# Pooling mixer of a decoder trunk: the 16 meta tokens as the last rows of a whole 128-token tile, and both halves of z scaled before the first pooled tile

## The chip, the cores and the metric

The kernel runs on one core of a Trainium2 chip. The metric is the device time in microseconds of one execution. Engines are named as the profile names them: PE is TensorE's matmul, PEld its weight load, DVE is VectorE, ACT is ScalarE, POOL is GpSimd, SP is SyncE. L558 is line 558 of the kernel before. PEclk is the clock that TensorE was granted, as a share of 2.4 GHz; it has two levels here, 1.00 (2.4 GHz) and 0.50 (1.2 GHz).

## What is computed

A trunk of two layers over 272 tokens of 1024 features: 256 tokens of the sequence and 16 learned meta tokens ahead of them, which are dropped at the end. Each layer is SwiGLU FFN, mixer, SwiGLU FFN, each with an RMS norm before and after it. The mixer of layer 0 is the causal pooling mixer, on which the change works:

```python
def causal_multiscale_pool(h, w, b, scale):
    cs = jnp.pad(jnp.cumsum(hf, axis=1), ((0, 0), (1, 0), (0, 0)))
    ...
    for g, win in enumerate(POOL_WINDOWS):          # 2, 4, 8, 16
        lo = jnp.maximum(t + 1 - win, 0)
        cnt = (t + 1 - lo).astype(jnp.float32)
        pooled.append((csg[:, 1:, g] - csg[:, lo, g]) / cnt[None, :, None])
    ...
    diff = (pooled - hg).astype(h.dtype)
    y = jnp.einsum('blgc,gcd->blgd', diff, w) + b   # four groups of 256 features
    return y.reshape(bsz, L, D) * scale
...
hn = rmsnorm(h, mix_norm_pre[i])
m = causal_multiscale_pool(hn, pool_w[j], pool_b[j], pool_scale[j])
h = h + rmsnorm(m, mix_norm_post[i])
```

The mixer of layer 1 is a differential attention, which the change leaves alone.

## The kernel before

The residual `h` stays on the chip, features on partitions: eight tiles `h[j]` of 128 features by 272 tokens. Columns 0 to 255 are the tokens of the sequence, columns 256 to 271 the 16 meta tokens, so that the meta tokens, first in time, stand last in a tile.

The order of work on PE, ACT, DVE and SP is written out by hand, and each engine runs its instructions in that order. Every stage follows the one before: FFN 0, the pooling mixer, FFN 1, FFN 2, the attention, FFN 3. An FFN has `first_blocks` (the first three of 22 blocks of the hidden layer, eight feature tiles one after the other, L416), the other up-products and the down-products (L216 to L218: each product in three passes over halves `hi` and `lo` of both operands). The weights are loaded by SP into `raw`, and ACT and DVE split them into `whi` (L101) and `wlo` (L114), some units ahead.

`pool_mix` works between FFN 0 and FFN 1, in full f32, where the trace shows two passes of PE for each product:

1. PE fills the time until the first `h[j]` with twelve products on constants (`warm`, L230), while DVE finishes the norm of FFN 0 and adds it to `h` (L569, L570).
2. `inner(j)`, L558: z = h^T w, for feature tile j and each token tile. Group g = j // 2 takes two tiles j. The token tiles are `tok`: columns 0 to 127, 128 to 255, and 256 to 271, so the third has 16 rows. `z[q][ti]` is a PSUM bank for half q of the features (j 0 to 3, j 4 to 7) and token tile ti. `inner(0)` to `inner(5)` come first, then L581, which sums the squares of each token into `sums` (three token tiles), then `inner(6)` and `inner(7)`.
3. `r2`: the reciprocal root of `sums`, in ACT (L242) and DVE (L236 to L238).
4. `normed(q)`: half q of z, scaled by r2 and copied into SBUF as `zs[0]` (ACT, L591), `zs[1]` (DVE, L592) and `zs[2]` (16 rows; ACT for q = 0, L596, DVE for q = 1, L594).
5. `pooled(j)`: PE multiplies columns j of `zs[1]`, `zs[0]` and `zs[2]` with the band matrices `bands` (L604, L605, L608) into one PSUM bank y of 128 features by 272 tokens. The third product has 16 rows of operand and writes the first 16 tokens and the meta tokens. ACT squares y (`post.squared`, L378), DVE sums the squares (L389). For j = 0, 3, 4 DVE also scales y at once (L371).
6. Three more `warm` products, then the norm's sum (`post.rms`, L395 and L396), its root (ACT, L242), and FFN 1 begins with L273 and L275 on DVE, which make the first operand `xhi`. The other scaled y are made by ACT then (L362, L373); that gives the banks free into which `first_blocks` writes.

What stands where in time is set by this loop, which the change replaces:

```python
for q in range(2):
    normed(q)
    for j in range(4 * q, 4 * q + 4):
        pooled(j)
        if j == 0:
            first(0)
        if j in EARLY:
            scaled(j, True)
```

Of the kernel before, what the change touches and what calls it, by code (L numbers as in the profile page):

```python
# [12 lines left out]
ALU = mybir.AluOpType  # L13
# [3 lines left out]
P = 128  # L17
D = 1024
NK = D // P
NMETA = 16  # L20
SEQ = 256
L = NMETA + SEQ
# [35 lines left out]
EARLY = (0, 3, 4)  # L58
# [86 lines left out]
def trunk(ctx, tc, ht, w13a, w13b, w2t, w2n, wqkva, wqkv, wo, wp, vec, lamv, mask, band, gpost, out):  # L145
    nc = tc.nc
# [11 lines left out]
    wps = []  # L158
# [381 lines left out]
    def pool_mix(old, ps, post):  # L540

        def bank():
            return ps.tile([P, 512], F32, tag="bank", name="bank")

        tok = ((0, P), (P, 2 * P), (2 * P, L))
        rows = (P, P, NMETA)

        z = [[bank() for _ in rows] for _ in range(2)]
        sums = bank()[:, 0:3]
        idle = bank()  # L550
        nc.vector.memset(sums, 0.0)
        warm(lambda: idle, ones, WARM0, P)
        old.refine()

        def inner(j):
            g = j // 2
            for ti, m in enumerate(rows):
                nc.tensor.matmul(z[g // 2][ti][:m, (g % 2) * 256:(g % 2 + 1) * 256],  # L558
                                 lhsT=h[j][:, tok[ti][0]:tok[ti][1]], rhs=wps[j], start=j % 2 == 0, stop=j % 2 == 1)

        with tc.tile_pool(name="poolw", bufs=1, reuse_waits="tile") as pw:
# [17 lines left out]
            nc.vector.tensor_tensor(acc[:, 0], acc[:, 0], acc[:, 1], ALU.add)  # L579
            for ti, m in enumerate(rows):  # L580
                nc.tensor.matmul(sums[:m, ti:ti + 1], lhsT=acc[:, 0, tok[ti][0]:tok[ti][1]], rhs=ones[:, 0:1],  # L581
                                 start=True, stop=True)
            for j in range(NK - LATE, NK):
# [5 lines left out]
            def normed(q):  # L589
                at = slice(q * 512, (q + 1) * 512)  # L590
                nc.scalar.mul(out=zs[0][:, at], in_=z[q][0], mul=r2[:, 0:1])  # L591
                nc.vector.tensor_scalar(zs[1][:, at], z[q][1], r2[:, 1:2], None, ALU.mult)  # L592
                if q:
                    nc.vector.tensor_scalar(zs[2][:NMETA, at], z[q][2][:NMETA], r2[:NMETA, 2:3], None, ALU.mult)  # L594
                else:
                    nc.scalar.mul(out=zs[2][:NMETA, at], in_=z[q][2][:NMETA], mul=r2[:NMETA, 2:3])  # L596

            def pooled(j):
# [8 lines left out]
                ends = y.rearrange("p (a b) -> p a b", b=SEQ)[:, :, 0:NMETA]  # L607
                nc.tensor.matmul(ends, lhsT=zs[2][:NMETA, c],  # L608
                                 rhs=bands[:NMETA, g, P + NMETA:].rearrange("p (a b) -> p a b", b=NMETA),
                                 start=False, stop=True, skip_group_check=True)  # L610
# [4 lines left out]
            def scaled(j, vector=False):  # L615
                post.scaled(j, ys[j][:, :L], pbg[:, j:j + 1], vector)

            def first(j):
                post.new(j, ys[j][:, :L], pfirst[:, j:j + 1], pfirst[:, NK + j:NK + j + 1])

            for q in range(2):
                normed(q)
                for j in range(4 * q, 4 * q + 4):
                    pooled(j)
                    if j == 0:
                        first(0)
                    if j in EARLY:
                        scaled(j, True)
            s = bank()
# [417 lines left out]
def _layout(x, meta_tokens, ffn_norm_pre, ffn_norm_post, ffn_w1, ffn_w3, ffn_w2, mix_norm_pre, mix_norm_post,  # L1047
# [9 lines left out]
    def first(a):  # L1057

        n = a.shape[0]
        a = a.transpose(0, 2, 1, 3, 4).reshape(n, P, 6, 8 * P)  # L1060
        return c(a.transpose(0, 2, 1, 3))
# [30 lines left out]
    ends = np.zeros((P, 4, 2 * NMETA))  # L1092
    ends[:NMETA] = np.where((d >= 0) & (d < win), 1.0 / count, 0.0) - (d == 0)
    r["band"] = c(np.concatenate([inside, ends], axis=2).astype(np.float32))
# [22 lines left out]
```

## Time and profile before

| | |
|---|---|
| three runs | 977.39, 979.08 and 979.39 us; median 979.08 us |
| profiled execution | 979.49 us, its span 977.4 us |
| PE busy | 958.1 us, 98% of the span |
| DVE, ACT busy | 602.7 us (62%), 500.4 us (51%) |
| mean granted clock of PE | 0.987 |
| HBM read | 158.56 MB, 163 GB/s over the span |

The busy times of the engines overlap, and a busy PE can be one at half its clock. The time of the execution is 2.1 us over its span.

### The profile page before, as it was taken

The page shows a single profiled execution, that of the slowest core. Times are in us where ns is not written, and L with a number is a line of the kernel's source. Part 1 is how long each engine was busy: PE and PEld are TensorE (multiplying, and loading weights), DVE is VectorE, ACT ScalarE, POOL GpSimd, SP SyncE. Part 2 cuts the span into 40 slices and gives each one's busy share as a digit, 9 for nine tenths or more (in the row PEclk, how much of TensorE's full clock was granted, in tenths as well). Part 3 has the DMA queues.
Part 4 walks back from the last instruction along what each step waited for, and adds up shares of the span by engine and source line. Part 5 has one row for each costly group of instructions (what it writes and reads, how often), then busy time and mean ns, then how long its engine had stood idle before and what let it go on. Part 6 is the DMA issues. An engine that isn't in the chain of part 4 may idle for free.

```text
span 977.4 us, 17910 instructions
## 1 busy us (share of the span) xinstructions
PE 958.1 (98%) x7242; PEld 923.0 (94%) x7242; DVE 602.7 (62%) x1029; ACT 500.4 (51%) x851; POOL 10.8 (1%) x18
## 2 busy tenths in 40 slices
PE   9999999998999999999999999999999999999997
PEld 8999999976999999999999999999997899999996
DVE  6855554453885555446955554458876788555553
ACT  7744454434564445543744455435776766444432
POOL 0000000200000000000000000000000000000000
PEclk9999999997899999999999999999999999999999
DMA  8765557630175556551665556532523538655521
GB/s 294 249 209 180 166 161 220 214 98 0 45 267 185 174 163 180 177 194 44 229 211 179 169 161 189 184 116 88 170 89 113 196 102 298 194 177 179 187 87 43
DMA packets 48322, 160.77 MB, mean 164 GB/s; under 512 B 5488, under 2 KB 9456, under 8 KB 48240
## 3 DMA queue, kind: packets, MB, share of 16 engines
q1 hardware_dynamic: 47952, 159.45, 50.8%
q8 instruction: 56, 0.92, 0.4%
q10 hardware_dynamic: 288, 0.19, 0.1%
q14 instruction: 26, 0.21, 0.1%
HBM read 158.56 MB, written 1.05 MB: 163 GB/s over the span
## 4 chain that ended last, share of the span: by engine, by line
PE 96%; ACT 1%; DVE 1%; DMA 1%; SPq 1%; issue 0%; DVEq 0%; ACTq 0%
PE bank L218 27%; PE bank L216 27%; PE bank L217 27%; PE bank L416 9%; PE bank L558 1%; DMA raw<-in_w13a 1%; PE bank L739 1%; ACT whi L101 0%; PE bank L604 0%; PE bank L230 0%; SPq L79 0%; PE bank L737 0%; PE bank L608 0%; PE bank L748 0%; PE bank L671 0%; PE bank L670 0%
## 5 line engine op out<-in xcount | busy, mean ns | idle before, releaser
L114 DVE TENSOR_TENSOR wlo<-raw,whi 128x1024 fp32r<-128x1024 f32 (+3 forms) x308 | 361.3, 1177 | 59.9 <-PE bank L217 28.3
L216 PE MATMUL bank<-xhi,whi 128*128 128x272 f32 (+1 forms) x1360 | 390.4, 287 | 0.0
L218 PE MATMUL bank<-xlo,whi 128*128 128x272 f32 (+1 forms) x1360 | 389.9, 287 | 0.0
L217 PE MATMUL bank<-xhi,wlo 128*128 128x272 f32 (+1 forms) x1360 | 388.6, 286 | 0.1
L101 ACT CAST whi<-raw 128x1024 fp32r<-128x1024 f32 (+3 forms) x308 | 306.7, 1011 | 54.9 <-PE bank L218 47.2
L216 PEld LDWEIGHTS bank<-xhi,whi 128*128 128x128 f32 x1360 | 255.8, 188 | 1.1 <-issue 0.4
L217 PEld LDWEIGHTS bank<-xhi,wlo 128*128 128x128 f32 x1360 | 255.7, 188 | 1.0 <-DVE wlo L114 0.3
L218 PEld LDWEIGHTS bank<-xlo,whi 128*128 128x128 f32 x1360 | 256.1, 188 | 0.0
L218 PE MATMUL bank<-glo,whi 128*128 128x272 f32 x528 | 152.3, 288 | 0.0
L216 PE MATMUL bank<-ghi,whi 128*128 128x272 f32 x528 | 152.1, 288 | 0.0
L217 PE MATMUL bank<-ghi,wlo 128*128 128x272 f32 x528 | 151.5, 287 | 0.0
L454 ACT ACTIVATE ua<-ua 128x272 f32<-128x272 f32 (+1 forms) x88 | 37.1, 429 | 143.5 <-DVE ua L449 143.5
L217 PEld LDWEIGHTS bank<-ghi,wlo 128*128 128x128 f32 x528 | 99.3, 188 | 0.0
L216 PEld LDWEIGHTS bank<-ghi,whi 128*128 128x128 f32 x528 | 99.2, 188 | 0.0
L218 PEld LDWEIGHTS bank<-glo,whi 128*128 128x128 f32 x528 | 99.0, 188 | 0.0
L460 DVE TENSOR_TENSOR ua<-bank,ua 128x272 f32<-128x272 f32 (+1 forms) x88 | 37.6, 435 | 95.0 <-PE bank L218 95.0
L463 ACT CAST ghi<-ua 128x272 fp32r<-128x272 f32 (+1 forms) x88 | 36.1, 417 | 112.0 <-DVE ua L460 112.0
L449 DVE TENSOR_TENSOR ua<-bank,ny 128x272 f32<-128x272 f32 (+1 forms) x88 | 37.6, 435 | 89.6 <-PE bank L218 89.5
L416 PE MATMUL bank<-xhi,whi 128*128 128x272 f32 (+1 forms) x240 | 40.5, 306 | 7.8 <-DVE xhi L275 6.2
L416 PEld LDWEIGHTS bank<-xhi,whi 128*128 128x128 f32 x240 | 34.9, 202 | 11.1 <-DVE xhi L275 6.3
L389 DVE TENSOR_TENSOR pacc<-pacc,sq 128x272 f32<-128x272 f32 (+1 forms) x31 | 13.6, 439 | 45.0 <-ACT sq L378 44.9
L378 ACT ACTIVATE sq<-bank 128x272 f32<-128x272 f32 (+1 forms) x32 | 12.8, 400 | 55.7 <-PE bank L218 55.7
(178 smaller groups left out, 894.1 us busy)
## 6 DMA issues: line engine op xcount, KB each, us to landing
raw<-in_w13b SPq DMA_DIRECT2D x152, 512.0 KB, 4.0
raw<-in_w2t SPq DMA_DIRECT2D x48, 448.0 KB, 3.3
raw<-in_w2t SPq DMA_DIRECT2D x24, 512.0 KB, 3.6
raw<-in_w2n SPq DMA_DIRECT2D x22, 512.0 KB, 3.5
raw<-in_w13a SPq DMA_DIRECT2D x21, 512.0 KB, 4.2
raw<-in_wqkv SPq DMA_DIRECT2D x18, 512.0 KB, 3.9
raw<-in_wo SPq DMA_DIRECT2D x8, 512.0 KB, 3.5
raw<-in_wqkva SPq DMA_DIRECT2D x6, 512.0 KB, 3.8
```

Source lines behind the costliest of these rows:

```text
L101: self.nc.scalar.copy(out=hi[:, at], in_=self.raws[u][:, at])
L114: self.nc.vector.tensor_tensor(lo[:, at], raw[:, at], hi[:, at].bitcast(F32), ALU.subtract)
L216: nc.tensor.matmul(out_ap, lhsT=a[0], rhs=b[0], start=start, stop=False)
L217: nc.tensor.matmul(out_ap, lhsT=a[1], rhs=b[0], start=False, stop=False)
L218: nc.tensor.matmul(out_ap, lhsT=a[0], rhs=b[1], start=False, stop=stop)
L378: nc.scalar.activation(out=sq[:, :n], in_=y, func=AF.Square, scale=scale, bias=bias)
L389: nc.vector.tensor_tensor(acc[:, :n], self.acc[:, :n], sq[:, :n], ALU.add)
L416: nc.tensor.matmul(us[q][:, :n], lhsT=taken[u][a][:, c * P:(c + 1) * P], rhs=x[:, :n], start=start, stop=stop)
L449: nc.vector.tensor_tensor(a[:, :self.n], u1[:, :self.n], self.r2[:, :self.n], ALU.mult)
L454: nc.scalar.activation(out=a[:, :self.n], in_=a[:, :self.n], func=AF.Silu)
L460: nc.vector.tensor_tensor(s[:, :n], u3[:, :n], s[:, :n], ALU.mult)
L463: nc.scalar.copy(out=hi, in_=s[:, :n])
```

## The change

The third token tile becomes columns 144 to 271, a whole tile of 128 tokens, of which the meta tokens are the last 16 rows. Its products in `inner` and its sums of squares have 128 rows in place of 16, its scaled copy `zs[2]` has 128 rows, and the third band product has 128 rows of operand. The band for it holds its values in rows 112 to 127, and zeros in the 112 rows above. The `memset` of `sums` goes. And `normed(0)` and `normed(1)` both stand ahead of the first `pooled(j)`, whose order stays.

```diff
-        tok = ((0, P), (P, 2 * P), (2 * P, L))
-        rows = (P, P, NMETA)
-
-        z = [[bank() for _ in rows] for _ in range(2)]
+        tok = ((0, P), (P, 2 * P), (L - P, L))
+
+        z = [[bank() for _ in tok] for _ in range(2)]
         sums = bank()[:, 0:3]
         idle = bank()
-        nc.vector.memset(sums, 0.0)
...
-            for ti, m in enumerate(rows):
-                nc.tensor.matmul(z[g // 2][ti][:m, (g % 2) * 256:(g % 2 + 1) * 256],
-                                 lhsT=h[j][:, tok[ti][0]:tok[ti][1]], rhs=wps[j], start=j % 2 == 0, stop=j % 2 == 1)
+            for ti, (t0, t1) in enumerate(tok):
+                nc.tensor.matmul(z[g // 2][ti][:, (g % 2) * 256:(g % 2 + 1) * 256],
+                                 lhsT=h[j][:, t0:t1], rhs=wps[j], start=j % 2 == 0, stop=j % 2 == 1)
...
-                    nc.vector.tensor_scalar(zs[2][:NMETA, at], z[q][2][:NMETA], r2[:NMETA, 2:3], None, ALU.mult)
+                    nc.vector.tensor_scalar(zs[2][:, at], z[q][2], r2[:, 2:3], None, ALU.mult)
                 else:
-                    nc.scalar.mul(out=zs[2][:NMETA, at], in_=z[q][2][:NMETA], mul=r2[:NMETA, 2:3])
+                    nc.scalar.mul(out=zs[2][:, at], in_=z[q][2], mul=r2[:, 2:3])
...
-                nc.tensor.matmul(ends, lhsT=zs[2][:NMETA, c],
-                                 rhs=bands[:NMETA, g, P + NMETA:].rearrange("p (a b) -> p a b", b=NMETA),
+                nc.tensor.matmul(ends, lhsT=zs[2][:, c],
+                                 rhs=bands[:, g, P + NMETA:].rearrange("p (a b) -> p a b", b=NMETA),
...
-            for q in range(2):
-                normed(q)
-                for j in range(4 * q, 4 * q + 4):
-                    pooled(j)
-                    if j == 0:
-                        first(0)
-                    if j in EARLY:
-                        scaled(j, True)
+            normed(0)
+            normed(1)
+            for j in range(NK):
+                pooled(j)
+                if j == 0:
+                    first(0)
+                if j in EARLY:
+                    scaled(j, True)
...
-    ends[:NMETA] = np.where((d >= 0) & (d < win), 1.0 / count, 0.0) - (d == 0)
+    ends[P - NMETA:] = np.where((d >= 0) & (d < win), 1.0 / count, 0.0) - (d == 0)
```

On PE, from the last token tile of `inner(5)` to the first pooled tile, the kernel before issues these (the size is that of the result, so 16x256 is a product for the meta tile; zs_2596 is `zs[1]`, zs_2595 `zs[0]`, zs_2597 `zs[2]`):

```order
L558 MATMUL bank<-wp,h 16x256
L581 MATMUL bank<-ones,pacc_2633 128x1 x2
L581 MATMUL bank<-ones,pacc_2633 16x1
L558 MATMUL bank<-wp,h 128x256 x2
L558 MATMUL bank<-wp,h 16x256
L558 MATMUL bank<-wp,h 128x256 x2
L558 MATMUL bank<-wp,h 16x256
L604 MATMUL bank<-bands,zs_2596 128x128
L605 MATMUL bank<-bands,zs_2595 128x144
L608 MATMUL bank<-bands,zs_2597 128x2x16
```

The changed kernel issues this from `inner(0)` to the first pooled tile (L557 is `inner`, L580 the sums, L602, L603 and L606 the band products, zs_2595 `zs[1]`, zs_2594 `zs[0]`, zs_2596 `zs[2]`):

```order
L557 MATMUL bank<-wp,h 128x256 x18
L580 MATMUL bank<-ones,pacc_2632 128x1 x3
L557 MATMUL bank<-wp,h 128x256 x6
L602 MATMUL bank<-bands,zs_2595 128x128
L603 MATMUL bank<-bands,zs_2594 128x144
L606 MATMUL bank<-bands,zs_2596 128x2x16
```

The number of products and their order are the same; no product with 16 rows or 16 result rows is left.

On DVE, from the root of the sums into the pooled tiles, before:

```order
L238 SCALAR_TENSOR_TENSOR ny<-nt,ny 128x3
L592 TENSOR_SCALAR zs_2596<-bank,ny 128x512
L371 TENSOR_SCALAR bt<-bank,psg,pbg 128x272
L389 TENSOR_TENSOR pacc<-sq 128x272
L389 TENSOR_TENSOR pacc<-pacc,sq 128x272
L371 TENSOR_SCALAR bt<-bank,psg,pbg 128x272
L592 TENSOR_SCALAR zs_2596<-bank,ny 128x512
L594 TENSOR_SCALAR zs_2597<-bank,ny 16x512
```

and in the changed kernel:

```order
L238 SCALAR_TENSOR_TENSOR ny<-nt,ny 128x3
L590 TENSOR_SCALAR zs_2595<-bank,ny 128x512 x2
L592 TENSOR_SCALAR zs_2596<-bank,ny 128x512
L371 TENSOR_SCALAR bt<-bank,psg,pbg 128x272
L389 TENSOR_TENSOR pacc<-sq 128x272
```

The two copies of half 1 (`zs[1]` and `zs[2]`) moved from behind two scaled tiles and two sums of squares to directly behind the copy of half 0.

On ACT, the same place before:

```order
L242 ACTIVATE ny<-bank,eps_c 128x3
L591 ACTIVATE zs_2595<-bank,ny 128x512
L596 ACTIVATE zs_2597<-bank,ny 16x512
L378 ACTIVATE sq<-bank,pbs,vt 128x272
L362 ACTIVATE b<-bank,pfirst 128x272
L378 ACTIVATE sq<-bank,pbs,vt 128x272 x3
L591 ACTIVATE zs_2595<-bank,ny 128x512
L378 ACTIVATE sq<-bank,pbs,vt 128x272 x4
```

and in the changed kernel:

```order
L242 ACTIVATE ny<-bank,eps_c 128x3
L589 ACTIVATE zs_2594<-bank,ny 128x512
L594 ACTIVATE zs_2596<-bank,ny 128x512
L589 ACTIVATE zs_2594<-bank,ny 128x512
L378 ACTIVATE sq<-bank,pbs,vt 128x272
L362 ACTIVATE b<-bank,pfirst 128x272
L378 ACTIVATE sq<-bank,pbs,vt 128x272 x7
```

The copy of half 1 moved from behind the fourth square to ahead of the first.

## Rows read from the trace of the kernel before

**Rows 1.** The page: the granted clock of PE in 40 equal slices of the span (tenths of full speed).

```profile
PEclk9999999997899999999999999999999999999999
```

**Rows 2.** Busy time of each engine by stretch, around the end of the mixer: the stretch, its length, busy us of PE, PEld, DVE, ACT and POOL (instructions), the granted clock, DMA share and GB/s.

```profile
225.00:230.00 5.00, 4.72 (x27) 3.36 (x26) 1.44 (x3) 2.45 (x5) 0.00 (x0) 1.00 0.00 0
230.00:235.00 5.00, 3.36 (x14) 2.81 (x15) 3.12 (x6) 1.81 (x4) 0.00 (x0) 0.74 0.00 2
240.00:245.00 5.00, 3.47 (x10) 2.03 (x8) 2.78 (x7) 3.40 (x8) 0.00 (x0) 0.50 0.00 0
245.00:250.00 5.00, 5.00 (x25) 5.00 (x25) 4.16 (x12) 2.06 (x5) 0.00 (x0) 0.55 0.02 3
```

**Rows 3.** The chain of work that ended last, in order of time, from the fourth pooled tile to the start of FFN 1: start, us, what.

```profile
229.75 0.59 ACT sq L378
...
230.37 0.56 DVE bt L371
230.93 0.67 DVE zs L592
...
231.64 0.49 PE bank L604 x2
...
241.60 0.50 ACT ny L242
...
242.12 0.45 DVE rt L273
...
242.60 0.45 DVE xhi L275
...
243.09 16.94 PE bank L416 x107
```

**Rows 4.** Timelines and groups of `inner`, L558. First PE: the start, length and number of passes of `inner(0)` to `inner(5)`; two passes of the second token tile's neighbourhood in `inner(1)`; the line's passes with shortest, median and longest ns. Then PEld, the weight loads of `inner(1)`, of which 128*16 is the meta tile's, with the idle time before them; and the loads of the whole stage by shape (busy us, mean ns, idle before).

```profile
212.24 9.62 PE L558 MATMUL bank<-wp,h 128*128 128x256 f32 x36 [0.46 <-issue]
...
214.13 0.59 PE L558 MATMUL bank<-wp,h 128*128 128x256 f32 x2
...
L558 PE MATMUL bank<-wp,h x48: 379/379/483, 212.2 to 225.3; 128*128 128x256 f32 x32, 128*16 128x256 f32 x16
...
214.87 0.11 PEld L558 LDWEIGHTS bank<-wp,h 128*16 128x16 f32 x2 [0.33 <-issue]
215.40 0.73 PEld L558 LDWEIGHTS bank<-wp,h 128*128 128x128 f32 x4 [0.42 <-issue]
...
L558 PEld LDWEIGHTS bank<-wp,h 128*128 128x128 f32 x32 | 5.4, 189 | 3.6 <-issue 3.2
L558 PEld LDWEIGHTS bank<-wp,h 128*16 128x16 f32 x16 | 0.9, 94 | 2.7 <-issue 2.7
```

**Rows 5.** Timeline of PE: the first product of pooled tiles 0, 1, 6 and 7, so that from row to row a whole tile of six passes lies between.

```profile
225.65 0.49 PE L604 MATMUL bank<-bands,zs 128*128 128x128 f32 x2
...
226.65 0.49 PE L604 MATMUL bank<-bands,zs 128*128 128x128 f32 x2
...
234.57 0.80 PE L604 MATMUL bank<-bands,zs 128*128 128x128 f32 x2
...
236.34 0.80 PE L604 MATMUL bank<-bands,zs 128*128 128x128 f32 x2
```

**Rows 6.** Timeline of PE at a granted clock of 1.00: the two products of a norm's sum, 24 passes of 128 columns on one weight shape, and the sums of squares (six passes of one column).

```profile
207.73 0.62 PE L395 MATMUL bank<-pacc,ones 128*128 128x272 f32 x2
208.38 0.73 PE L396 MATMUL bank<-sq,ones 128*128 128x272 f32 x2
208.94 2.84 PE L230 MATMUL bank<-ones 128*128 128x128 f32 x24
...
221.79 0.74 PE L581 MATMUL bank<-ones,pacc 128*128 128x1 f32 x6
```

**Rows 7.** Timelines of DVE and ACT around the first copies of z.

```profile
219.22 0.44 DVE L579 TENSOR_TENSOR pacc<-pacc 128x272 f32<-128x272 f32 x1
...
231.50 0.73 DVE L594 TENSOR_SCALAR zs<-bank,ny 16x512 f32<-16x512 f32 x1
...
223.52 0.69 ACT L591 ACTIVATE zs<-bank,ny 128x512 f32<-128x512 f32 x1 [0.69 <-DVE ny L238]
224.10 0.66 ACT L596 ACTIVATE zs<-bank,ny 16x512 f32<-16x512 f32 x1
```

**Rows 8.** `first_blocks` (L416) of FFN 1 and of FFN 2: the passes of its last kind, with ns shortest, median, longest, and first and last start in us. Then the last of FFN 1's first six weight loads, with the idle time before it.

```profile
L416 PE MATMUL bank<-xlo,whi x48: 283/288/289, 252.5 to 264.9; 128*128 128x272 f32 x48
...
L416 PE MATMUL bank<-xlo,whi x48: 283/288/289, 454.8 to 467.2; 128*128 128x272 f32 x48
...
244.96 0.29 PEld L416 LDWEIGHTS bank<-xhi,whi 128*128 128x128 f32 x1 [0.19 <-ACT bt L373]
```

**Rows 9.** The same seam between two other stages. First PE's first product of FFN 2 with the idle time before it, and the stretch around it; then those of FFN 3 and the stretch behind its start (columns as in rows 2).

```profile
448.69 0.52 PE L416 MATMUL bank<-xhi,whi 128*128 128x272 f32 x2 [1.55 <-DVE xhi L275]
447.10:450.50 3.40, 1.85 (x15) 1.81 (x15) 2.67 (x7) 0.97 (x3) 0.00 (x0) 1.00 0.00 0
...
781.13 0.96 PE L416 MATMUL bank<-xhi,whi 128*128 128x256 f32 x6 [1.62 <-DVE xhi L275]
782.00:785.40 3.40, 3.03 (x15) 2.73 (x15) 3.09 (x9) 1.24 (x3) 0.00 (x0) 0.51 0.27 110
```

**Rows 10.** A stretch of FFN 1 behind its `first_blocks` (columns as in rows 2).

```profile
265.00:300.00 35.00, 35.00 (x281) 35.00 (x280) 28.44 (x44) 22.47 (x35) 0.00 (x0) 1.00 0.68 227
```

More of the change, by code (lines that the diff above doesn't have):

```diff
@@ L579, in pool_mix @@
             nc.vector.tensor_tensor(acc[:, 0], acc[:, 0], acc[:, 1], ALU.add)
-            for ti, m in enumerate(rows):
-                nc.tensor.matmul(sums[:m, ti:ti + 1], lhsT=acc[:, 0, tok[ti][0]:tok[ti][1]], rhs=ones[:, 0:1],
-                                 start=True, stop=True)
+            for ti, (t0, t1) in enumerate(tok):
+                nc.tensor.matmul(sums[:, ti:ti + 1], lhsT=acc[:, 0, t0:t1], rhs=ones[:, 0:1], start=True, stop=True)
             for j in range(NK - LATE, NK):
```

## Prediction, made before the changed kernel was run

> **What bounds the kernel now.** I read the page's clock row first. PE's granted clock is full almost everywhere, with one dent in slices 10 and 11, at 220 to 269 us, which is the mixer's end [rows 1]. The stretches there say when: 1.00 to 230, 0.74 in 230 to 235, 0.50 to 245, 0.55 in 245 to 250 [rows 2]. Those are the two levels of 2.4 and 1.2 GHz. Next I read the chain: elsewhere it runs through PE, but at 229.75 it leaves PE for 1.9 us. The square of tile 3 on ACT, a scaled tile on DVE (L371) and then the copy of z's second half (L592) end before PE starts tile 4 at 231.64 [rows 3]. So PE waits for a copy whose input was long there, since it stands behind other work on its engine. The clock falls right behind that idle stretch, and stays low until FFN 1's products run.
>
> The mixer's products cost more than their columns. Six `inner` products run from 212.24 [rows 4] to the sums' start at 221.79 [rows 6], 1.59 us each. Two neighbouring full passes together take 0.59 us, one alone 0.38, so their starts lie 0.21 us apart; six at that pace are 1.29. The missing 0.30 us lie at the meta tile. Its load begins after 0.33 us in which PEld idles, and the load of the next full tile after 0.42 [rows 4]: PE lets nothing overlap where it goes from 128 rows to 16 or back. A pooled tile, with one 16-row product among three, takes 1.00 us [rows 5].
>
> **The change, part by part.**
>
> *Full tiles in `inner`.* The count of products stays, and so does their column count of 256. What a full third tile costs is bounded below by 1.29 us a product (all six passes at 0.21) and above by 1.59 plus the dearer loads, 2 x (189 - 94) ns = 0.19 [rows 4]. I take 1.29, since two full tiles in a row show it, with their loads hidden. Eight products gain 8 x 0.30 = 2.4 us. What else could hold PE: the sums need the squares' total, which DVE ends at 219.66 [rows 7], and PE now arrives at 221.79 - 6 x 0.30 = 220.0. Cover remains, 0.3 us.
>
> A rule of the Trainium skill speaks against this part: in TensorE: Matmul & The Clock Gate, section LDWEIGHTS (loading the stationary operand), a load's time goes by its columns, about columns / 1.2 ns, so that 16 to 128 adds 93 ns to a load. The trace's 94 and 189 ns agree with that difference [rows 4]. By the rule alone, 16 loads would add an estimated 1.5 us where I subtract 2.4.
>
> *Full rows in the pooled tiles.* Bounds for a tile: 1.00 us if nothing goes, and below that six passes at the pace of passes with full loads. 24 constant passes of 128 columns take 2.84 us, so at most 0.118 each with the last one's tail in it, and passes of one column are no closer (0.74 us for six) [rows 6]; I take 0.112 a pass. Six passes, two of them with 144 columns (0.125), are 0.70. I take 0.70: 8 x 0.30 = 2.4 us.
>
> *Copies with 128 partitions.* ACT takes 0.66 us for 16 partitions and 0.69 for 128 [rows 7]: nothing. They must be there when PE comes. From the sums' start to the first copy is 223.52 - 221.79 = 1.73 us, so the copy starts at 221.73, ACT's second one 0.58 later, and ends 0.69 after that, at 223.0 [rows 6, 7]. PE reaches tile 0 at 225.65 - 2.4 = 223.25 [rows 5]. 0.25 us of cover; without it the lateness would count in full.
>
> *Half 1 scaled first.* The stall goes: four tiles of 1.00 from 225.65 end at 229.65, and PE went on at 231.64, so 2.0 us [rows 3, 5]. Behind `inner(7)`, at 223.25, DVE makes both copies of half 1 in about 0.73 us each [rows 7], to 224.7; tile 4 needs them at 223.25 + 4 x 0.70 = 226.05. What queues behind them: ACT's first square waits until its copy ends, near 223.95, which is when tile 0 is finished anyway. DVE's first scaled tile and sums move 1.5 us, and have all the tiles to catch up. The `memset` lay in an idle stretch of DVE: nothing.
>
> *The clock.* Without that stall PE works from 212.24 to the norm's sum with no wait that I can find. So I take 1.00 until there. Before, from tile 4 at 231.64 to the root at 241.60 [rows 3] is 9.96 us. At full clock, with 1.00 a tile, that is 4 x 1.00, 0.67 for six constant passes at 0.112, and at most 1.38 for the norm's sum (207.73 to 209.11, with a short wait in it; I take 1.3) [rows 6]: 5.97. The gain is 4.0 us. The drop itself shows in the tiles: 1.77 us at 234.57 against 1.00 [rows 5].
>
> *FFN 1's first blocks.* From 243.09 [rows 3] to 264.9 they take 21.8 us, in FFN 2 at full clock 448.69 [rows 9] to 467.2, 18.5 [rows 8]. Not all of the 3.3 comes back: FFN 1's first six passes need banks that ACT frees (the last load 1.87 us after the start, behind `bt` of L373 [rows 8], where six passes at 18.5 / 143 = 0.13 would need 0.65). That 1.2 us is ACT's and stays. Gain 2.1.
>
> *Sum.* 2.4 + 2.4 + 2.0 + 4.0 = 10.8 us up to FFN 1's first product, which comes at 232.3 in place of 243.09 (the root, 1.49 us ahead of it, is unchanged work [rows 3]), and 2.1 behind it: 12.9 us. FFN 1 can take it: in 265 to 300, PE never idles, and DVE and ACT, which prepare its weights, are busy 28.4 and 22.5 of 35 us [rows 10]. Against the profiled 979.49 that makes 966.6 us; the median of the three runs is 0.4 lower than that execution.
>
> What stays open is the seam into FFN 1, where PE idles about 1.5 us and then waits 1.2 us more in pieces. The seam into FFN 2 idles 1.55 us at a clock of 1.00; the seam into FFN 3 idles 1.62 and then shows 0.51 for 3.4 us [rows 9]. So such a seam goes either way, at a price of at most half of 3.4, 1.7 us. I give a fall at FFN 1's seam one half, and one half to FFN 3's fall being absent. The two cancel but for a little: 966.8 us. No fall at either gives 964.9, a fall at both 968.3. The likeliest case has 965 to 968.5.
>
> **The rivals.**
>
> *The switch costs what it did.* If the lost 0.30 us belong to the third product as such and not to its 16 rows, 4.8 us stay: 971.4 us. For it: no run shows the changed shape. Against it: nothing is lost between the two full tiles. 0.08. If in addition the load's time is not hidden, as it would be were the rule of LDWEIGHTS the whole bill, but the pooled tiles gain theirs (their loads have 128 columns already), `inner` costs 16 x 0.095 = 1.5 more instead of 2.4 less: 966.6 + 3.9 = 970.5. Against it: PEld idles between loads of 189 ns. 0.04.
>
> *The clock falls all the same.* The pooled tiles are short products, and at full clock without drains they might not hold it. At half clock from 223.25 on, tiles, constants and norm cost up to their 7.6 us once more, and the first blocks keep their 2.1: 966.6 + 9.7 = 976.3. For it: once low, the clock stayed low under them. Against it: 1.00 in 225 to 230 under the same tiles [rows 2]. 0.05.
>
> *The stall moves.* If tile 0 came to wait for half 1's copies, PE would idle about 1.5 us at 223.25 instead of 2.0 at 229.65, and the clock could fall behind it as before. Drains and 0.5 us gained: about 974.2. Against it: in the changed kernel only tile 4 uses half 1. 0.03.
>
> *Slower.* The clock falls ahead of the sums. A faster `inner` runs closer behind DVE, and PE may wait there for `h` and then for the squares' total, with 0.3 us of cover now. Work at 1.2 GHz costs twice. From the sums at 220.0 to the norm's root PE has 10.8 us of work, so a fall there takes all 10.8 back, and with the first blocks' 2.1 the time is 979.5, as before. That is the point from which it decides: a fall earlier is slower by as much as PE works before 220.0, 987.3 for one at the first product. Against it: the waits there are tenths, and 0.46 us of idle ahead of 212.24 [rows 4] left the clock at full. 0.02, half of it slower.
>
> **How the numbers follow.** The likeliest case has 0.78. The range takes in the nearest rival, 970.5, and some error of the paces below: 964.6 to 971.0, which leaves out about 0.18. A measurement of this kernel tells about 0.2% (2.0 us) from no change. All but the last rival lie under 977.1, so faster has 0.96; same and slower have 0.02 each, the last rival and what I do not see.
>
> **What would show it.** `inner` at 1.29 us a product and tiles at 0.70, with no idle of PEld ahead of the third tile's loads; tile 4 directly behind tile 3; a granted clock of 1.00 through the norm's sum; FFN 1's first product near 232.3 and its blocks near 19.7 us. Wrong would be: tiles still at 1.00, a wait for `zs` at tile 0, or 0.50 before 230.

## The result, and the profile after

The changed kernel takes **965.91 us** (median; 965.41 to 967.24) against 978.7 us for the kernel before in the same comparison (977.39 to 979.39): ratio 0.9871, 95% interval 0.9859 to 0.9884. The profiled execution took 965.49 us, with a span of 963.6 us where it was 977.4. The instructions of the mixer stand one or two lines higher now: `inner` L557, the sums of squares L580, the band products L602, L603 and L606, the copies of z L589, L590, L592 and L594.

The page, with its clock row (before: [rows 1]):

```profile
span 963.6 us, 17909 instructions
PEclk9999999999999999999999999999999999999999
```

The dent in slices 10 and 11 is gone. By stretch (columns as in [rows 2]):

```profile
225.00:230.00 5.00, 4.99 (x40) 4.72 (x40) 3.73 (x9) 3.59 (x7) 0.00 (x0) 1.00 0.00 0
230.00:235.00 5.00, 3.15 (x15) 2.04 (x15) 3.73 (x10) 3.77 (x8) 0.00 (x0) 0.96 0.01 3
235.00:240.00 5.00, 5.00 (x31) 5.00 (x31) 4.33 (x12) 2.12 (x5) 0.00 (x0) 0.70 0.00 0
```

A fall is left, but a short one and in another place: 0.96 and 0.70 amount to 0.4 + 3.0 = 3.4 us at half clock (the shortfall times 5 us, over 0.5), inside FFN 1's first blocks. Before, the same sum over 230 to 250 (0.50 in 235 to 240) gives 17.1 us.

PE's timeline of the mixer (start, length, operation, passes, idle time before):

```profile
211.67 8.11 PE L557 MATMUL bank<-wp,h 128*128 128x256 f32 x36 [0.46 <-issue]
219.62 0.72 PE L580 MATMUL bank<-ones,pacc 128*128 128x1 f32 x6
220.20 2.84 PE L557 MATMUL bank<-wp,h 128*128 128x256 f32 x12
222.88 0.38 PE L602 MATMUL bank<-bands,zs 128*128 128x128 f32 x2
...
224.87 0.47 PE L602 MATMUL bank<-bands,zs 128*128 128x128 f32 x2
...
225.56 0.47 PE L602 MATMUL bank<-bands,zs 128*128 128x128 f32 x2
...
228.32 0.91 PE L230 MATMUL bank<-ones 128*128 128x128 f32 x6
...
229.82 0.62 PE L396 MATMUL bank<-sq,ones 128*128 128x272 f32 x2
232.06 2.16 PE L416 MATMUL bank<-xhi,whi 128*128 128x272 f32 x6 [1.62 <-DVE xhi L275]
```

There is one group of 36 passes of `inner` and no row with an idle time from there to FFN 1. Six products take 219.62 - 211.67 = 7.95 us, 1.325 each. A tile takes 0.69 us (224.87 to 225.56), and tile 4, at 225.56, stands directly behind tile 3. The weight loads of `inner` show why:

```profile
213.03 6.34 PEld L557 LDWEIGHTS bank<-wp,h 128*128 128x128 f32 x30 [0.23 <-issue]
```

30 loads stand in one stretch of 6.34 us. In [rows 4] PEld idled 0.33 us ahead of each meta tile's loads and 0.42 behind them. The copies of half 1 on DVE, and the root on ACT:

```profile
222.64 0.75 DVE L590 TENSOR_SCALAR zs<-bank,ny 128x512 f32<-128x512 f32 x1 [0.56 <-PE bank L557]
223.31 0.74 DVE L592 TENSOR_SCALAR zs<-bank,ny 128x512 f32<-128x512 f32 x1
```

```profile
230.48 0.49 ACT L242 ACTIVATE ny<-bank,eps_c 128x272 f32<-128x272 f32 x1 [1.32 <-PE bank L396]
```

The copies end at 224.05, 1.5 us before tile 4 wants them; before, the one with which tile 4 begins ended at 231.60 [rows 3], and PE waited for it.

**Where the time went.** The starts of the rows above against those of [rows 3 to 6], stretch by stretch:

| stretch | before, us | after, us | gain | forecast |
|---|---|---|---|---|
| span's start to the first product of `inner` | 212.24 | 211.67 | 0.57 | 0 |
| to tile 0 (`inner`, sums) | 13.41 | 11.21 | 2.20 | 2.4 |
| to tile 4 (four tiles, stall) | 5.99 | 2.68 | 3.31 | 1.2 + 2.0 |
| to the norm's root | 9.96 | 4.92 | 5.04 | 1.2 + 4.0 |
| to FFN 1's first product | 1.49 | 1.58 | -0.09 | 0 |
| FFN 1's first blocks | 21.8 | 21.1 | 0.7 | 2.1, less a possible fall |
| from there to the attention's last first block | 405.0 | 405.1 | -0.1 | 0 |
| the attention from its last first block to FFN 3 | 111.2 | 109.6 | 1.6 | 0 |
| FFN 3 to the span's end | 196.3 | 195.6 | 0.7 | 0 to 1.7 |

The gains add up to the span's 13.8 us but for rounding. The 0.57 us at the start do not belong to the change: in the twelve profiled executions of this document `inner` begins at 211.31 to 212.27 us, at 211.40 in one with the old tiles and at 212.27 in one with the new. The 0.7 us of FFN 3 lie in its first blocks, and the clock at their start explains them: 0.51 for 3.4 us before [rows 9], 1.00 after.

```profile
768.80:772.20 3.40, 2.44 (x20) 2.23 (x19) 3.09 (x9) 1.24 (x3) 0.00 (x0) 1.00 0.26 102
```

The attention was not in the forecast at all. The ends of the first blocks ahead of it, of the kernel before and then of the changed one (first and last start):

```profile
L416 PE MATMUL bank<-xlo,whi x48: 278/287/291, 657.1 to 669.9; 128*128 128x272 f32 x32, 128*128 128x256 f32 x16
```

```profile
L416 PE MATMUL bank<-xlo,whi x48: 278/287/291, 645.5 to 658.3; 128*128 128x272 f32 x32, 128*128 128x256 f32 x16
```

and FFN 3's first product, at 781.13 before [rows 9], now:

```profile
767.94 0.95 PE L416 MATMUL bank<-xhi,whi 128*128 128x256 f32 x6 [1.62 <-DVE xhi L275]
```

781.13 - 669.9 = 111.2, 767.94 - 658.3 = 109.6. Not one instruction of that stage is changed. The two timelines of PE part at the first output product, first the kernel before, then the changed one:

```profile
751.51 0.38 PE L216 MATMUL bank<-ohi,whi 128*128 128x256 f32 x1 [1.34 <-ACT am L730]
```

```profile
738.34 0.36 PE L216 MATMUL bank<-ohi,whi 128*128 128x256 f32 x1
```

Before, that product idled 1.34 us for ACT's copy `am`, which it does not read. What is left for it to wait for is the PSUM bank into which it writes, and the runs with other banks (below) bear this out. In the changed kernel it follows without an idle.

### The profile page after: what moved, and what is told of

It is laid out like the page before. It is cut to its first block, busy times and chain, and to the rows that moved or that the text cites. A ratio compares the mean times of both kernels' runs of the same rounds, so it can differ in the third digit from the quotient of the medians.

```text
span 963.6 us, 17909 instructions
## 1 busy us (share of the span) xinstructions
PE 946.7 (98%) x7242; PEld 919.1 (95%) x7242; DVE 602.4 (63%) x1028; ACT 500.2 (52%) x851; POOL 10.8 (1%) x18
## 4 chain that ended last, share of the span: by engine, by line
PE 96%; ACT 1%; DMA 1%; DVE 1%; issue 0%; SPq 0%; DVEq 0%; ACTq 0%
PE bank L218 27%; PE bank L217 27%; PE bank L216 27%; PE bank L416 9%; PE bank L557 1%; DMA raw<-in_w13a 1%; PE bank L737 1%; ACT whi L101 0%; PE bank L746 0%; PE bank L735 0%; PE bank L230 0%; PE bank L669 0%; PE bank L668 0%; PE bank L602 0%; PE bank L603 0%
## 5 line engine op out<-in xcount | busy, mean ns | idle before, releaser
L416 PE MATMUL bank<-xhi,whi 128*128 128x272 f32 (+1 forms) x240 | 38.9, 296 | 8.5 <-DVE xhi L275 6.3
L416 PEld LDWEIGHTS bank<-xhi,whi 128*128 128x128 f32 x240 | 33.4, 194 | 11.5 <-issue 4.0
```

Of the source, the lines that this page charges most:

```text
L416: nc.tensor.matmul(us[q][:, :n], lhsT=taken[u][a][:, c * P:(c + 1) * P], rhs=x[:, :n], start=start, stop=stop)
```

## The experiments

The theory has three parts. **A**: the stall ahead of tile 4 lets the clock fall, and what stands behind it pays; rival **B**: the thin tiles themselves let it fall. **C**: PE loses time where neighbouring products have 128 and 16 rows, and not by what a third tile costs as such. **D**, formed after the result: the attention's 1.6 us come from the rotation of banks. Ratios are to the kernel before on the same chip.

**Order alone.** The kernel before, with its 16-row tiles:

```diff
-            for q in range(2):
-                normed(q)
-                for j in range(4 * q, 4 * q + 4):
-                    pooled(j)
...
+            normed(0)
+            normed(1)
+            for j in range(NK):
+                pooled(j)
...
```

> The kernel before with one edit: both halves of z are scaled ahead of the first pooled tile; the meta tile keeps its 16 rows. Theory A (three separate causes: drains at the 16-row products, the stall behind tile 3, and a clock that falls because of that stall): inner stays at 1.59 us a product, the pooled tiles at 1.00 us, all eight in a row, and the granted clock stays 1.00 through them. Against the changed kernel (965.9) the drains' 4.8 us come back: about 970.7 us, 7 to 9 us under the kernel before. Rival B (the clock falls because the pooled tiles are thin, stall or no stall): 0.50 before the norm's sum, tiles of 1.77 us, and 975 us or more.

Measured: 973.48 us, ratio 0.9937 (0.9921 to 0.9954). Tile 0, what stands behind tile 7, and FFN 1's first product; then two stretches across the tiles and the seam; then the attention's first output product:

```profile
224.81 0.49 PE L604 MATMUL bank<-bands,zs 128*128 128x128 f32 x2
...
232.81 0.94 PE L230 MATMUL bank<-ones 128*128 128x128 f32 x6
...
236.28 2.21 PE L416 MATMUL bank<-xhi,whi 128*128 128x272 f32 x6 [1.62 <-DVE xhi L275]
```

```profile
230.00:235.00 5.00, 4.66 (x28) 3.60 (x27) 2.23 (x6) 2.59 (x5) 0.00 (x0) 1.00 0.00 0
235.00:240.00 5.00, 3.48 (x14) 2.81 (x15) 4.47 (x11) 3.47 (x8) 0.00 (x0) 0.82 0.01 3
```

```profile
745.24 0.38 PE L216 MATMUL bank<-ohi,whi 128*128 128x256 f32 x1 [0.99 <-DVE nt L237]
```

All eight thin tiles run at 1.00 us each (224.81 to 232.81) and at full clock; the 0.82 belongs to FFN 1's first blocks. So A and not B: without the stall, the thin tiles do not let the clock fall. From tile 0 to FFN 1's first product it is 11.47 us where it was 17.44 [rows 3, 5]: the 5.97 us between them are the forecast's 6.0 for stall and clock. The whole time is 2.8 us over A's number. That number was reckoned from the changed kernel and so had the fall at FFN 1's seam in it; what it did not have are a fall of 3.4 us at the attention's seam, about 1.5 us, and the wait of 0.99 us above, with which the attention's stretch takes 110.9 us (664.0 to 774.9) in place of 109.6.

**Tiles alone.** The changed kernel with the old loop:

```diff
-            normed(0)
-            normed(1)
-            for j in range(NK):
-                pooled(j)
...
+            for q in range(2):
+                normed(q)
+                for j in range(4 * q, 4 * q + 4):
+                    pooled(j)
...
```

> The changed kernel with one edit undone: half 1 of z is scaled behind pooled tile 3 again; the meta tile is 128 rows. Theory A: inner at 1.29 us, tiles 0 to 3 at 0.69, then PE idles about 2 us ahead of tile 4, and the clock falls to 0.50 within some us of it, until FFN 1's products run. Stall 2.0, and tiles 4 to 7, the constants and the norm's sum (5.0 us of work at full clock) once more, and some 1 us in the first blocks: about 973.5 us. Rival B (the stall does no harm to the clock; it was the drains that made the stretch thin): 965.9 + 2.0 = 968 us, the clock at 1.00 to the seam.

Measured: 969.59 us, ratio 0.9902 (0.9888 to 0.9917). PE behind the stall, and the stretches:

```profile
228.26 0.69 PE L602 MATMUL bank<-bands,zs 128*128 128x128 f32 x2 [1.93 <-DVE zs L590]
...
229.51 0.78 PE L602 MATMUL bank<-bands,zs 128*128 128x128 f32 x2
230.85 0.77 PE L602 MATMUL bank<-bands,zs 128*128 128x128 f32 x2
...
232.00 0.47 PE L602 MATMUL bank<-bands,zs 128*128 128x128 f32 x2
```

```profile
225.00:230.00 5.00, 3.07 (x20) 2.96 (x20) 3.57 (x7) 2.66 (x6) 0.00 (x0) 0.84 0.00 2
230.00:235.00 5.00, 4.54 (x28) 4.03 (x26) 1.79 (x4) 2.53 (x6) 0.00 (x0) 0.82 0.00 0
```

The stall is back, and the clock falls behind it, as A has it: tile 5 takes 1.34 us (229.51 to 230.85). But it is up again by tile 7, after 1.6 + 1.8 = 3.4 us. With the 16-row tiles it stayed low for 17.1 us in the kernel before, and for some 10 us in the kernel before with other banks (below). A's number, 973.5, had taken the long low over from there, and is refuted by 3.9 us. That the full tiles are what makes the low short is not shown: one mixer gave both 17.1 and some 10 us, the 3.4 us are from one execution, and the mean clock of this kernel's other three (0.994, 0.992 and 0.992, against 0.995) leaves room for a longer low there.

The two parts of the change overlap. In the profiled executions it is, from the first product of `inner` to that of FFN 1, 30.85 us before, 24.88 with the order alone (211.40 to 236.28), 23.80 with the tiles alone (212.27 to 236.07) and 20.39 with both. The gains of 5.97 and 7.05 us make 13.02, and both together 10.46, since each by itself takes away most of the low clock.

**Third tile of 64 rows, and of 80 rows.** The changed kernel but for the rows (16 meta tokens behind 48 or 64 tokens that the second tile also has, with zeros in the bands), and with the `memset` of `sums` back, which the changed kernel had dropped:

```diff
-        tok = ((0, P), (P, 2 * P), (L - P, L))
+        tok = ((0, P), (P, 2 * P), (L - 64, L))
...
+        nc.vector.memset(sums, 0.0)
...
-                nc.tensor.matmul(ends, lhsT=zs[2][:, c],
-                                 rhs=bands[:, g, P + NMETA:].rearrange("p (a b) -> p a b", b=NMETA),
+                nc.tensor.matmul(ends, lhsT=zs[2][:64, c],
+                                 rhs=bands[:64, g, P + NMETA:].rearrange("p (a b) -> p a b", b=NMETA),
```

> The changed kernel with a third token tile of 64 rows (columns 208 to 271) in place of 128, the meta tokens still its last 16, in inner, the sums, the scaled copy and the pooled products. It asks what of the whole tile counts. Theory C (PE drains where the size of the used part of the array changes, and parts of 64 rows or less are another size): PEld idles ahead of the third tile's loads as it did with 16 rows, inner at 1.59 us, tiles near 1.00: about 970.7 us. Rival D (only a very thin tile costs, or the bare number of weight columns): between, near 966 to 968 us.

> The changed kernel with a third token tile of 80 rows (columns 192 to 271). Theory C (80 rows take the whole array as 128 do): nothing drains, inner at 1.29 us, tiles at 0.69, and 965.9 us as the changed kernel, so that the tile need not be whole. Rival E (any tile short of 128 rows drains): 970.7 us, as with 16 or 64.

Measured: 64 rows 971.77 us, ratio 0.9924 (0.9909 to 0.9938); 80 rows 967.68 us, ratio 0.9877 (0.9862 to 0.9891). Loads of `inner` and two tiles with 64 rows:

```profile
212.77 0.19 PEld L558 LDWEIGHTS bank<-wp,h 128*64 128x64 f32 x2 [0.33 <-issue]
213.34 0.73 PEld L558 LDWEIGHTS bank<-wp,h 128*128 128x128 f32 x4 [0.39 <-issue]
```

```profile
226.54 0.49 PE L603 MATMUL bank<-bands,zs 128*128 128x128 f32 x2
...
227.54 0.49 PE L603 MATMUL bank<-bands,zs 128*128 128x128 f32 x2
```

and with 80 rows:

```profile
224.12 0.47 PE L603 MATMUL bank<-bands,zs 128*128 128x128 f32 x2
...
224.67 0.31 PE L607 MATMUL bank<-bands,zs 80*128 80x32 f32 x2
224.81 0.47 PE L603 MATMUL bank<-bands,zs 128*128 128x128 f32 x2
...
739.52 0.39 PE L216 MATMUL bank<-ohi,whi 128*128 128x256 f32 x1 [0.99 <-DVE nt L237]
```

With 64 rows the idles of 0.33 and 0.39 us stand where they stood with 16, and a tile takes 1.00 us; with 80 it takes 0.69, though the tile is no more whole than the other. C holds, and it is sharper than the forecast had it: what costs is not a tile that is not full, but one of 16 or 64 rows between full ones (between 64 and 80 nothing was tried). In `inner` these rows of the result are the columns of the loaded operand (128*64 above), in a pooled tile they are its rows (80*128); both cost much the same. The Trainium skill, TensorEngine Tiling (Array Packing), section Key Properties, has a rule that fits: changing the tiling mode drains TensorE, and its section Available Configurations has modes of 128, 64 and 32 rows and of 128, 64 and 32 columns. The trace agrees, with 0.27 us in `inner` and 0.31 in a tile for a switch there and back, though no row tells the mode of a product.

Both times lie above C's numbers, by 1.1 and 1.8 us. Of this 1.2 are the attention's: its first output product waits again, by 0.99 us in either trace (the last row above), and its stretch is 110.8 us in place of 109.6.

**The stall filled.** The kernel before, with nine constant products in it and nothing else:

```diff
                 normed(q)
+                if q:
+                    fill = bank()
+                    warm(lambda: fill, ones, 9, P)
                 for j in range(4 * q, 4 * q + 4):
```

> The kernel before with one addition: nine products on constants (18 passes of 128 columns, 2.0 us at full clock, their result unused) stand between pooled tiles 3 and 4, so that PE works through the 1.9 us in which it waits for half 1 of z. Stall and drains stay. Theory A (the idle stretch lets the clock fall): tiles 4 to 7 at 1.00 us and a granted clock of 1.00 to the seam; the 4.0 us there and 0.6 to 2.1 us in the first blocks are gained: 972.6 to 974.1 us against 978.7. Rival B (thin tiles let it fall): the clock still goes to 0.50 ahead of the norm's sum, and the time stays within 1 us of 978.7.

Measured: 974.36 us, ratio 0.9956 (0.9942 to 0.997). PE around the filling:

```profile
228.84 2.27 PE L230 MATMUL bank<-ones 128*128 128x128 f32 x18
230.96 0.43 PE L604 MATMUL bank<-bands,zs 128*128 128x128 f32 x2
231.90 0.49 PE L604 MATMUL bank<-bands,zs 128*128 128x128 f32 x2
...
238.28 1.99 PE L416 MATMUL bank<-xhi,whi 128*128 128x272 f32 x5 [1.53 <-DVE xhi L275]
```

Tile 4 comes no earlier by it than the wait for its copy allows, and it takes 0.94 us, where a tile behind the stall took 1.77 [rows 5]. This shows the clock's share alone: the idle stretch, and not the lateness, is what lets it fall. From tile 0 (224.85) to FFN 1's first product it is 13.43 us in place of 17.44, which is the forecast's 4.0. The whole time is 0.3 us over the expected range; here too the clock fell for 3.4 us at the attention's seam.

**Other banks.** The kernel before, and the changed kernel, with the pools of the output banks in another order; no instruction moves:

```diff
-YORDER = (2, 0, 1, 3)
+YORDER = (3, 0, 1, 2)
```

> The kernel before with one line changed, YORDER = (3, 0, 1, 2): in the attention's output stage its results lie in PSUM banks of another order. The mixer is untouched. The two traces differ by 1.55 us at one place far from the change: the kernel before has PE idle 1.34 us ahead of the first output product of the attention (751.5 us, behind the copy am of ACT), the changed one has not. Theory F (the mixer's bank requests shift which bank that product gets, and in the kernel before it is one that ACT frees late): with another bank the idle stretch is gone, and the time is 1.5 us under the kernel before, 977.2. Rival G (chance or a DMA): the idle stretch stays, 978.7 us.

> The changed kernel with YORDER = (3, 0, 1, 2) alone, which moves no instruction: the bank of the first output product of the attention is then the one that ScalarE's last copy at (L727, ends at 739.0 + 0.46 = about 739.5 in the changed kernel's trace) frees, where the product now starts at 738.34 without an idle. Theory D (1.59 us of the gain came from the rotation of the PSUM banks and not from the pooling mixer): an idle of 1.0 to 1.3 us in front of that product is back, the stretch of the attention is 110.6 to 110.9 us rather than 109.6, and the time is 1.0 to 1.3 us over the changed kernel's 965.9: about 967.1. Rival: TensorE waits for the heads' later steps anyway and the 1.59 us came from something else, say the clock: time and stretch as in the changed kernel, 965.9 and 109.6.

Measured: the kernel before with it 977.99 us, ratio 0.9992 (0.9981 to 1.0003); the changed kernel with it 966.91 us, ratio 0.9878 (0.9861 to 0.9894). The first output product, of the kernel before with it, then of the changed kernel with it:

```profile
750.20 0.36 PE L216 MATMUL bank<-ohi,whi 128*128 128x256 f32 x1
```

```profile
739.31 0.38 PE L216 MATMUL bank<-ohi,whi 128*128 128x256 f32 x1 [1.07 <-ACT at L727]
```

In the kernel before with it, the mixer's stall stands as ever, and the low clock behind it is what was set beside the full tiles above:

```profile
230.00:235.00 5.00, 3.70 (x13) 3.02 (x14) 3.12 (x6) 1.21 (x3) 0.00 (x0) 0.51 0.00 0
235.00:240.00 5.00, 5.00 (x19) 4.32 (x20) 0.88 (x2) 1.68 (x3) 0.00 (x0) 0.50 0.00 0
```

The idle of the output product goes in the one and comes in the other, and the attention's stretch goes with it: 109.6 us (670.2 to 779.8) and 110.9 (658.0 to 768.94). So the traces bear D out in both directions. Which part of the edit turns the rotation, the other runs narrow down. The three kernels with the new order and the `memset`, with 16, 64 and 80 rows, all wait 0.99 us at that product, and the kernel before, with the old order and the `memset`, 1.34 us. The two without the `memset` do not wait, with the new order (the changed kernel) or the old one (tiles alone, a stretch of 109.6 us):

```profile
742.41 0.36 PE L216 MATMUL bank<-ohi,whi 128*128 128x256 f32 x1
```

So the order does not take the wait away, and the `memset` may be what counts; it was not removed by itself. The whole times do not settle what D is worth: 1.0 us more in the changed kernel, as expected, but its interval overlaps the changed kernel's own, and the 0.08% in the kernel before is within its interval of nothing.

**The seam into FFN 1 filled.** The changed kernel with six constant products behind the norm's sum:

```diff
             post.rms(lambda: s, True)
+            fill = bank()
+            warm(lambda: fill, ones, 6, P)
```

> The changed kernel with six products on constants (12 passes, 1.34 us, result unused) behind the norm's sum, where PE idles 1.6 us ahead of FFN 1's first product. Theory H (the idle stretch and the thin start behind it are what lets the clock fall there in the changed kernel, 0.70 in 235 to 240): no fall at that seam, first blocks of 19.7 us in place of 21.2, 964.5 us. Rival I (the wait for the banks behind it is enough to let it fall, or the fill delays the first product): 965.9 or more.

Measured: 965.33 us, ratio 0.9859 (0.9838 to 0.988), not to be told from the changed kernel. PE there, with the stretch behind it, and the same length behind FFN 2's start:

```profile
230.53 1.50 PE L230 MATMUL bank<-ones 128*128 128x128 f32 x12
232.31 2.16 PE L416 MATMUL bank<-xhi,whi 128*128 128x272 f32 x6 [0.28 <-DVE xhi L275]
```

```profile
234.60:238.00 3.40, 3.40 (x29) 3.40 (x29) 2.98 (x8) 1.13 (x3) 0.00 (x0) 1.00 0.00 0
...
436.70:440.10 3.40, 3.40 (x17) 3.40 (x17) 3.14 (x8) 0.41 (x1) 0.00 (x0) 0.51 0.00 0
```

The fall at FFN 1 is gone: its first blocks take 19.7 us in place of 21.1, so such a fall costs about 1.5 us. But FFN 2's seam, at 1.00 in the kernel before [rows 9] and in the changed one, has one now, and pays the same. That is the profiled execution; the five times fall into two groups, 963.5 and 964.0 us at a mean clock of 0.998, and 965.3 to 966.2 at 0.996 and 0.997, so that it need not have fallen in all. Whether the filling sent it there is open: in two profiled executions without a filling, that with 64 rows and that of the changed kernel with other banks, the fall stood at FFN 2's seam too (first blocks of 20.0 us there and 19.7 at FFN 1's).

**The banks of FFN 1 freed early as well.** As the last one, and the scalings `first(1)` and `first(2)` of ACT stand ahead of the norm's sum, so that ACT comes to `bt` (L373) earlier:

```diff
                     scaled(j, True)
+            for j in range(1, post.ahead):
+                first(j)
             s = bank()
...
             warm(lambda: fill, ones, 6, P)
-            for j in range(1, post.ahead):
-                first(j)
```

> As the kernel with six fill products, and ACT makes the two scaled tiles that FFN 1 needs first (first(1), first(2)) in the 1.3 us in which it waits for the norm's sum, ahead of the root in place of behind it; the bt tiles that free the banks then come 0.95 us earlier. Theory H: the first six passes of the first blocks take about 1.0 us in place of 1.9, on top of the fill: 963.5 us. Rival I: the clock and PE's own pace hide it, 964.5 us as with the fill alone.

Measured: 964.33 us, ratio 0.9852 (0.9834 to 0.9871). FFN 1's first six passes:

```profile
232.01 1.22 PE L416 MATMUL bank<-xhi,whi 128*128 128x272 f32 x6 [0.28 <-DVE xhi L275]
```

From there to the next group 1.06 us, where it was 2.0; the first blocks take 18.7 us. FFN 2's seam falls again (20.0 us there). The time lies at the rival's 964.5. It is 1.0 us under that of the last kernel, as the theory and the trace have it, but the intervals overlap, so the times alone do not settle it.

**All seams filled.** As the last one, with the same six products at the seams into FFN 2, the attention and FFN 3:

```diff
-YORDER = (2, 0, 1, 3)
+YORDER = (3, 0, 1, 2)
...
             post.rms(bank, False, RMS_REFILL[i])
+            if i:
+                fill = bank()
+                warm(lambda: fill, ones, 6, P)
...
         post.rms(bank_of[0], True, 1)
+        fill = bank_of[0]()
+        warm(lambda: fill, ones, 6, P)
```

> e8_both6 with six constant products more behind the sums at the seams of FFN 1, FFN 2 and the attention as well (one clause in ffn() for i = 1, 2, one in attn_out()), and YORDER = (3, 0, 1, 2), since two more banks shift the rotation and the first output product of the attention would otherwise wait for the late copy. If the fall of the clock in e7_seam6 and e8_both6 only moved on to the next seam that was not filled, no seam is left for it: 1.5 us less at FFN 2's seam (first blocks 18.5 rather than 20.03), granted clock 1.00 from the warm-up to the last norm, 964.3 - 1.5 = about 962.8. Rival: the fills themselves take as long as the fall costs, or the clock falls at a place that is not a seam: 964 to 965.

Measured: 963.75 us (963.67 to 965.29), ratio 0.9848 (0.9833 to 0.9863). FFN 2's seam, and the attention's first output product:

```profile
435.60:439.00 3.40, 3.40 (x29) 3.40 (x28) 3.02 (x8) 0.84 (x2) 0.00 (x0) 1.00 0.00 0
```

```profile
736.77 0.39 PE L216 MATMUL bank<-ohi,whi 128*128 128x256 f32 x1 [1.00 <-DVE nt L237]
```

No seam falls in the profiled execution: 1.5 us are gained at FFN 2's (18.55 us there). The fillings do not rule a fall out, though: three of the four executions took 963.67 to 963.77 us at a mean clock of 0.999, and the fourth 965.29 at 0.996. 1.2 us are lost again in the attention, where two more banks have turned the rotation, and the order of pools chosen against it leaves a wait of 1.00 us. This explains 963.75 where 962.8 was expected. It is the fastest kernel here: every time of it is below every time of the changed kernel (965.29 against 965.41), though the two were timed on different occasions and the intervals of their ratios overlap by 0.0004.

## Why the prediction was right, and where it was not

966.8 us were forecast and 965.91 measured. That the total came so near is in part luck: 2.2 us came from places that no term names (0.57 at the start, 1.6 in the attention), and 1.4 of the first blocks' 2.1 did not come. The terms up to FFN 1 held. Step by step:

- **Drains in `inner`**: 2.4 forecast, 2.20 measured. The pace is 1.325 us a product rather than 1.29; a pass in a row of full ones takes 0.22 us, not 0.21 (six at 0.21 would be 1.26, not the 1.29 that the text has). That the loads would cost nothing holds: 190 ns each, hidden behind passes of 0.22.
- **Pooled tiles**: 0.70 us forecast, 0.69 measured; 2.4 us gained. The 64- and 80-row runs show that it is the change between full and thin products, and not a third product as such.
- **Stall and clock**: 2.0 and 4.0 forecast. Taking the tiles' 2.4 off, the two stretches give 3.31 + 5.04 - 2.4 = 5.95. The run with the stall filled and the one with the order alone show that the stall lets the clock fall, and give the sizes: 4.0 us with the stall filled, 5.97 with it gone. That the clock stays low until FFN 1's products run did not hold elsewhere: with other banks the kernel before was at 1.00 again from 240.4, ahead of FFN 1's first product at 242.70, and with the tiles alone by tile 7.
- **FFN 1's first product**: 232.3 forecast, 232.06 measured, of which 0.57 is the earlier start; counted from `inner`'s first product, 10.46 of the 10.8 us came.
- **First blocks**: 2.1 forecast as the term, 0.7 measured. The clock fell at the seam, to which the text gave one half, and that took the rest. Without a fall the forecast had 19.7 us, and the run with the filled seam shows 19.7. The 1.2 us of waiting it left to ACT's `bt` are real: 0.9 of them go when ACT comes to it earlier.
- **The seams**: the forecast gave halves to FFN 1's and FFN 3's and took FFN 2's for safe, on one trace with 1.55 us of idle at 1.00. In each profiled execution here with unfilled seams the clock was low behind one of the two seams ahead of FFN 1 and FFN 2 and not behind the other (in the kernel before it was low there already). FFN 3's fell in that of the kernel before alone, and cost 0.7 us, where the forecast allowed up to 1.7. The attention's, which the forecast does not weigh, fell in three kernels with 16-row tiles (order alone, stall filled, other banks).
- **The attention**: the step that is missing. "FFN 1 can take it" and what follows were taken as shifted as they are. 1.6 us came from a bank that is handed out otherwise. The `memset` was counted at nothing, because it lay in an idle stretch of DVE; the wait at the output product goes with it, as far as the runs tell. This gain and the missing 1.4 us of the first blocks nearly cancel.

Left open: what decides at which of several seams with about 1.6 us of idle the clock falls (in the kernels with FFN 1's filled it stood at FFN 2's, in others without a filling too), what sets how long it then stays low, and whether the `memset` by itself turns the rotation of the banks, and how.

## What to carry to other kernels

Look for a product of few rows between full ones: if its loads are preceded and followed by idle of PEld, padding it (here 80 rows did, 64 did not) is worth the idle, here about 0.3 us each time, and costs nothing as long as the loads stay hidden. Price an idle of PE by the clock of the stretch behind it, not by its length: 2 us of waiting cost 6. After an edit that adds or removes a PSUM tile or an instruction that uses one, or moves its last reader, compare every later stage's first write into a bank with its releaser, since a rotation can gain or lose more than a microsecond two stages away.

## What was not expected of the hardware

- 64 rows drain as 16 do (1.00 us a tile), 80 rows do not (0.69 us).
- Behind the same stall of about 2 us the clock stayed low for 17.1 us and for some 10 us in two kernels with the same mixer, and for 3.4 us in one with full tiles (one execution of each).
- Each fall at a seam lasted 3.4 us; at FFN 1's, FFN 2's and the attention's it cost about 1.5, at FFN 3's 0.7. With 1.50 us of constant products at FFN 1's seam alone it stood at FFN 2's, 200 us later, in the profiled executions of both kernels; with all seams filled it stood at none in the profiled one.
